# One large add with GELU: the arrays as three blocks in sequence, with an input parked in another's place

## The chip, the core and the metric

The kernel runs on one core of a Trainium2 chip. The inputs and the output lie in HBM; the core's compute engines read and write SBUF, an on-chip memory of 128 partitions, and 16 DMA engines move data between the two. Engines that matter here: DVE (VectorE) adds, ACT (ScalarE) computes the GELU, SP (SyncE) issues the transfers, POOL (GpSimd) takes part in the barriers and clears semaphores at the end.

The metric is the time of one execution on the device, in microseconds (us). The kernel before was run three times: 120.11 us median, 120.04 to 120.16.

## The reference

Two float32 arrays of 1024 x 4096 (16.78 MB each) are added, and the tanh form of the GELU is taken of each sum:

```python
def reference(x, y):
    z = x + y
    return (0.5 * z * (1 + np.tanh(np.sqrt(2 / np.pi) * (z + 0.044715 * z ** 3)))).astype(np.float32)
```

Every output element depends on the same element of x and of y alone. So any split of the elements into rows and blocks is allowed, if x, y and the output are split alike.

## The kernel before

**Tiling.** Each array is seen as 128 rows of TOT = 32,768 elements (8 rows of the array one after the other, 128 KB), one for each partition. The tile `zt` (128 x 32,768) holds x, then the sum, then the result, all in place. The tile `yt` (128 x 16,384) holds one half of y at a time; the second half of y goes where the first one was.

**Transfers.** All of them are issued by SP, in one queue, in the order of the list `sp`: the first half of y (64 KB a row), both halves of x (64 KB each), then the second half of y in two pieces (48 and 16 KB a row), then the two halves of the output (64 KB each). The functions are `load_x` (L123), `load_y` (L128) and `store` (L132). Seven transfers, each of 128 rows, eight rows for each of the 16 DMA engines.

**Compute.** The elements are cut into 17 chunks (`chunks`): fifteen of 2,048 and two of 1,024 elements a partition. `add` (L151) does x + y on DVE, `gelu` (L156) does the activation in place on ACT.

**Order.** The program is written out by hand inside `tc.manual_schedule()`: a loop takes from the lists `sp`, `acts` and `dve` whatever has its needs done already (`needs`), and so sets each engine's own order. Across engines only semaphores hold. The waits that matter on SP:

- the 48 KB piece of y waits for the first six adds, as it overwrites what they read; the 16 KB piece waits for the eighth;
- the first store waits for the eight gelus of the first half, and by the constant `GATE = 8` (L96) also for the ninth add, the first of the second half. That dependency is added by hand (L134) with the reason "the stores join the queue when the last load is nearly done";
- the second store waits for the last gelu.

Two edits of the finished instruction list frame this. `begin_early` moves the first two transfers on SP ahead of the barrier with which the program starts. `wait_late` takes the wait for the last transfer out of the closing barrier, so that the reset of the semaphores is done while the last store is still under way; ACT waits for that store alone, as the very last instruction.

A one-element GELU at the start (L183) loads ACT's table while the first loads run.

Of the kernel before, what the change touches and what calls it, by code (L numbers as in the profile page):

```python
# [8 lines left out]
def begin_early(nc, count):  # L9


    head, body = (b.instructions for b in nc.main_func.blocks[:2])
    SP = mybir.EngineType.SP
    moved = [i for i in body if i.engine == SP and isinstance(i, mybir.InstDMACopy)][:count]
    assert not any(i.sync_info and i.sync_info.on_wait for i in moved)
    assert all(i.regs_accessed() == ((), ()) for i in moved)
    at = next(k for k, i in enumerate(head) if i.engine == SP)
    for k, i in enumerate(moved):
        body.remove(i)
        head.insert(at + k, i)  # L20


def wait_late(nc):

    body, end = (b.instructions for b in nc.main_func.blocks[1:3])
    last = [i for i in body if isinstance(i, mybir.InstDMACopy)][-1]
    (sem,) = [u.id for u in last.sync_info.on_update]
    all_done = end[0]  # L30
    reset = next(i for i in end if isinstance(i, mybir.InstDrain) and i.is_reset_sema)
    at = end.index(reset)
    clear = end[at + 1]
    first, stop = reset.reset_range_start, reset.reset_range_stop
    assert all_done.engine == mybir.EngineType.SP and reset.engine == mybir.EngineType.Pool
    assert isinstance(clear, mybir.InstISA) and clear.engine == mybir.EngineType.Pool
    waits = all_done.sync_info.on_wait
    (its,) = [w for w in waits if w.id == sem]

    end[0] = mybir.InstDrain(  # L40
        name=all_done.name, engine=all_done.engine, debug=all_done.debug, is_reset_sema=False,
        sync_info=mybir.SyncInfo(on_wait=[w for w in waits if w.id != sem], on_update=[]),
    )
    parts = []
    for f, e in ((first, sem), (sem + 1, stop)):
        if f < e:
            nc.gpsimd.sem_clear(range(f, e))
            parts.append(nc.cur_bb.bb.instructions.pop())
    end[at + 1 : at + 2] = parts
    end.append(  # L50
        mybir.InstEventSemaphore(
            name=clear.name, engine=mybir.EngineType.Activation, debug=clear.debug,
            sync_info=mybir.SyncInfo(
                on_wait=[its],
                on_update=[
                    mybir.SyncUpdate(
                        sync_type="semaphore", id=sem, ant_name=its.ant_name,
                        update_mode="sem-sub-imm", update_value=its.wait_value,
                    )
                ],  # L60
            ),
        )
    )


@with_exitstack
def kernel(
    ctx: ExitStack,
    tc: tile.TileContext,
    x: bass.AP,  # L70
    y: bass.AP,
    out: bass.AP,
):

    nc = tc.nc
    P = nc.NUM_PARTITIONS  # L80
    fp32 = mybir.dt.float32
    act = mybir.ActivationFunctionType

    N, D = x.shape
    assert N % P == 0
    TOT = N // P * D
    xv, yv, ov = (a.rearrange("(p n) d -> p (n d)", p=P) for a in (x, y, out))

    HALF = TOT // 2
    xloads = [HALF, HALF]  # L90
    yloads = [16384, 12288, 4096]
    stores = [16384, 16384]
    chunks = [2048] * 15 + [1024, 1024]
    by_pool = []
    in_psum = []
    GATE = 8  # L96

    def ranges(sizes):
        ends = [sum(sizes[: i + 1]) for i in range(len(sizes))]
        assert ends[-1] == TOT  # L100
        return [(e - f, e) for e, f in zip(ends, sizes)]

    xr, yr, sr, cr = (ranges(r) for r in (xloads, yloads, stores, chunks))
    C = len(cr)
    second = next(c for c in range(C) if cr[c][0] == HALF)

    def over(rs, lo, hi):
        return [i for i, (a, b) in enumerate(rs) if a < hi and b > lo]

    pool_sb = ctx.enter_context(tc.tile_pool(name="xz", bufs=1))  # L110
    pool_y = ctx.enter_context(tc.tile_pool(name="y", bufs=1))
    pool_ps = ctx.enter_context(
        tc.tile_pool(name="ps", bufs=max(1, len(in_psum)), space=bass.MemoryType.PSUM)
    )

    one = pool_sb.tile([P, 992], fp32, tag="one", name="one")
    zt = pool_sb.tile([P, TOT], fp32, tag="z", name="z")
    yt = pool_y.tile([P, HALF], fp32, tag="y", name="y")
    xp, adds = {}, {}

    def load_x(i):
        a, b = xr[i]
        nc.sync.dma_start(out=zt[:, a:b], in_=xv[:, a:b])  # L123

    def load_y(i):
        a, b = yr[i]
        o = a % HALF
        nc.sync.dma_start(out=yt[:, o : o + b - a], in_=yv[:, a:b])  # L128

    def store(i):  # L130
        a, b = sr[i]
        ins = nc.sync.dma_start(out=ov[:, a:b], in_=zt[:, a:b])  # L132
        if i == 0 and GATE is not None:
            tc.add_manual_dep(  # L134
                ins.ins,
                adds[GATE].name,
                mybir.DependencyInfo(mybir.DependencyClass.Sync, mybir.DependencyReason.DATA),
                reason="the stores join the queue when the last load is nearly done",
            )

    def to_psum(c):
        a, b = cr[c]
        xp[c] = pool_ps.tile([P, 2048], fp32, tag="xp", name=f"xp{c}")
        nc.scalar.copy(out=xp[c][:, : b - a], in_=zt[:, a:b])

    def add(c):
        a, b = cr[c]
        o = a % HALF
        eng = nc.gpsimd if c in by_pool else nc.vector
        first = xp[c][:, : b - a] if c in in_psum else zt[:, a:b]  # L150
        ins = eng.tensor_add(out=zt[:, a:b], in0=first, in1=yt[:, o : o + b - a])  # L151
        adds[c] = ins.ins

    def gelu(c):
        a, b = cr[c]
        nc.scalar.activation(out=zt[:, a:b], in_=zt[:, a:b], func=act.Gelu_apprx_tanh)  # L156

    sp = [(load_y, i) for i in over(yr, 0, HALF)] + [(load_x, 0), (load_x, 1)]
    sp += [(load_y, i) for i in over(yr, HALF, TOT)]
    sp += [(store, i) for i in range(len(stores))]  # L160
    pool = [(add, c) for c in by_pool]
    dve = [(add, c) for c in range(C) if c not in by_pool]
    order = list(range(second, C))
    acts = [(gelu, c) for c in range(second)] + [(to_psum, c) for c in in_psum]
    acts += [(gelu, c) for c in order]
    assert sorted(order) == list(range(second, C))

    needs = {
        load_x: lambda i: [],
        load_y: lambda i: [(add, c) for c in over(cr, yr[i][0] - HALF, yr[i][1] - HALF)],  # L170
        to_psum: lambda c: [(load_x, i) for i in over(xr, *cr[c])],
        add: lambda c: [(load_x, i) for i in over(xr, *cr[c])]
        + [(load_y, i) for i in over(yr, *cr[c])]
        + [(to_psum, k) for k in in_psum if k == c],
        gelu: lambda c: [(add, c)],
        store: lambda i: [(gelu, c) for c in over(cr, *sr[i])]
        + ([(add, GATE)] if GATE is not None else []),
    }
    queues = [sp, pool, acts, dve]
    done = set()  # L180
    with tc.manual_schedule():
        nc.vector.memset(one[:, :1], 0.0)  # L182
        nc.scalar.activation(out=one[:, :1], in_=one[:, :1], func=act.Gelu_apprx_tanh)  # L183
        while any(queues):
            moved = False
            for q in queues:
                while q and all(n in done for n in needs[q[0][0]](q[0][1])):
                    fn, arg = q.pop(0)
                    fn(arg)
                    done.add((fn, arg))  # L190
                    moved = True
                    if q is not sp:
                        break
            assert moved, [q[:1] for q in queues]

    ctx.close()
    tc.close()
    tc.compile()  # L198
    begin_early(nc, 2)
    wait_late(nc)  # L200
# [30 lines left out]
```

## Time and profile before

One execution was profiled. Its own time and what else matters:

| | us |
|---|---|
| the profiled execution's own time | 120.19 |
| its span, from the first to the last of the program's instructions | 118.7 |
| DVE busy, 18 instructions | 35.5 |
| ACT busy, 19 instructions | 32.0 |
| idle time of DVE before its adds, ended by a landing of x | 40.0 |
| the same, ended by a landing of y | 16.2 |
| one add of 128 x 2,048, mean | 2.285 |
| one GELU of 128 x 2,048, mean | 1.910 |
| DMA engines' share of the span with packets | 98.5% |

How to read the profile: a line such as L151 is a line of the kernel's source. "SPq" is SP's sequencer, which waits and issues transfers. `z<-in_x_dram` is what an operation writes and reads, by the program's names. The row of digits for DMA has the span in 40 equal slices and gives the busy share of the 16 DMA engines in each, in tenths (9 is 90% or more). The trace also records every DMA packet with its start, duration and size; in this kernel one packet is one row of a transfer, and one more packet of 4 bytes for each DMA engine closes a transfer.

### The profile page before, as it was taken

The page shows a single profiled execution, that of the slowest core. Times are in us where ns is not written, and L with a number is a line of the kernel's source. Part 1 is how long each engine was busy: PE and PEld are TensorE (multiplying, and loading weights), DVE is VectorE, ACT ScalarE, POOL GpSimd, SP SyncE. Part 2 cuts the span into 40 slices and gives each one's busy share as a digit, 9 for nine tenths or more (in the row PEclk, how much of TensorE's full clock was granted, in tenths as well). Part 3 has the DMA queues.
Part 4 walks back from the last instruction along what each step waited for, and adds up shares of the span by engine and source line. Part 5 has one row for each costly group of instructions (what it writes and reads, how often), then busy time and mean ns, then how long its engine had stood idle before and what let it go on. Part 6 is the DMA issues. An engine that isn't in the chain of part 4 may idle for free.

```text
span 118.7 us, 96 instructions
## 1 busy us (share of the span) xinstructions
DVE 35.5 (30%) x18; ACT 32.0 (27%) x19; POOL 0.2 (0%) x4
## 2 busy tenths in 40 slices
DVE  0000000000000099999900000699999300000000
ACT  5000000000000029899850000079989800000000
POOL 0000000000000000000000000000000000000000
DMA  9889888998899888988898996998899889988890
GB/s 353 353 353 685 375 353 353 596 464 353 353 442 618 353 353 353 685 375 353 353 530 381 414 530 271 431 624 353 353 596 464 353 353 442 618 353 353 353 685 22
DMA packets 1008, 50.33 MB, mean 424 GB/s; under 512 B 112, under 2 KB 112, under 8 KB 112
## 3 DMA queue, kind: packets, MB, share of 16 engines
q1 hardware_dynamic: 1008, 50.33, 98.5%
HBM read 33.55 MB, written 16.78 MB: 424 GB/s over the span
## 4 chain that ended last, share of the span: by engine, by line
DMA 52%; DVE 22%; ACT 2%; DVEq 2%; ACTq 1%; SPq 0%; issue 0%
DMA z<-in_x_dram 34%; DVE z L151 22%; DMA y<-in_y_dram 17%; ACT z L156 2%; DVEq L198 2%; ACTq L198 1%; SPq L128 0%; DVEq L151 0%
## 5 line engine op out<-in xcount | busy, mean ns | idle before, releaser
L151 DVE TENSOR_TENSOR z<-z,y 128x2048 f32<-128x2048 f32 (+1 forms) x17 | 35.5, 2160 | 56.2 <-DMA z<-in_x_dram 40.0
L156 ACT ACTIVATE z<-z 128x2048 f32<-128x2048 f32 (+1 forms) x17 | 30.5, 1807 | 61.3 <-DVE z L151 61.3
L183 ACT ACT_TABLE_LOAD x1 | 1.3, 1283 | 1.3 <-PEq L215 1.3
L182 DVE MEMSET one<- 128x1 f32 x1 | 0.1, 59 | 1.3 <-PEq L215 1.3
L183 ACT ACTIVATE one<-one 128x1 f32<-128x1 f32 x1 | 0.2, 203 | 0.0
L215 POOL MEMSET const-bfloat16-1.0<- 128x1 bf16 x1 | 0.1, 101 | 0.0
L215 POOL MEMSET const-uint8-127<- 128x1 uint8 x1 | 0.1, 101 | 0.0
L215 POOL MEMSET const-float32-0.0<- 128x1 f32 x1 | 0.1, 98 | 0.2 <-issue 0.2
L215 POOL MEMSET const-float32-1.0<- 128x1 f32 x1 | 0.1, 98 | 0.0
## 6 DMA issues: line engine op xcount, KB each, us to landing
y<-in_y_dram SPq DMA_DIRECT2D x1, 6144.0 KB, 20.5
y<-in_y_dram SPq DMA_DIRECT2D x1, 2048.0 KB, 20.9
z<-in_x_dram SPq DMA_DIRECT2D x2, 50.1
out_dram<-z SPq DMA_DIRECT2D x2, 22.9
y<-in_y_dram SPq DMA_DIRECT2D x1, 22.0
```

Source lines behind the costliest of these rows:

```text
L151: ins = eng.tensor_add(out=zt[:, a:b], in0=first, in1=yt[:, o : o + b - a])
L156: nc.scalar.activation(out=zt[:, a:b], in_=zt[:, a:b], func=act.Gelu_apprx_tanh)
L182: nc.vector.memset(one[:, :1], 0.0)
L183: nc.scalar.activation(out=one[:, :1], in_=one[:, :1], func=act.Gelu_apprx_tanh)
L198: tc.compile()
L215: nc = _bacc.Bacc("TRN2", target_bir_lowering=False, num_devices=1)
```

## The change

The arrays are flattened, and cut into three blocks that follow each other in HBM. Block k is 128 rows of `LEN[k]` elements: 12,544, 7,680 and 12,544 (50,176, 30,720 and 50,176 bytes a row). A row goes to one partition. A transfer of a block thus covers one unbroken stretch of HBM, where before it took a piece out of each of 128 rows that lie 128 KB apart.

`yt` has room for y of blocks 1 and 2. y of block 0 is loaded into the place in `zt` that x of block 2 takes later (`y_at`). So y and x of block 0, x of block 1 and y of block 2 can be issued at once; x of block 2 waits until the seven adds of block 0 have read the parked y. Blocks are computed in the order 0, 2, 1, with seven, four (block 1) and seven pieces of 1,792, 1,920 and 1,792 elements. The stores are issued in the order 0, 2, 1; the first one also waits for the third add of block 2 (`GATE = (2, 2)`). Nine transfers replace seven.

In the instruction lists, SP's order becomes: y0, x0 (both ahead of the barrier), x1, y2, then x2 with a wait for DVE and for the landing of y0, y1, then the three stores with their waits. DVE has 18 adds where it had 17, ACT 18 gelus where it had 17. POOL clears its semaphores at the end with two instructions instead of one, since the semaphore of the last store no longer lies at the end of the range. `begin_early` and `wait_late` are unchanged.

```diff
-    xv, yv, ov = (a.rearrange("(p n) d -> p (n d)", p=P) for a in (x, y, out))
+    LEN = [12544, 7680, 12544]
+    PIECES = [7, 4, 7]
+    GATE = (2, 2)
+    AT = [sum(LEN[:k]) for k in range(3)]
-    xloads = [HALF, HALF]
-    yloads = [16384, 12288, 4096]
-    stores = [16384, 16384]
-    chunks = [2048] * 15 + [1024, 1024]
-    GATE = 8
+    def rows(a, k):
+        flat = a.rearrange("n d -> (n d)")
+        return flat[P * AT[k] : P * (AT[k] + LEN[k])].rearrange("(p c) -> p c", p=P)
...
     zt = pool_sb.tile([P, TOT], fp32, tag="z", name="z")
-    yt = pool_y.tile([P, HALF], fp32, tag="y", name="y")
+    yt = pool_sb.tile([P, LEN[1] + LEN[2]], fp32, tag="y", name="y")
+    def z(k, lo=0, hi=None):
+        return zt[:, AT[k] + lo : AT[k] + (LEN[k] if hi is None else hi)]
+    def y_at(k, lo=0, hi=None):
+        hi = LEN[k] if hi is None else hi
+        if k == 0:
+            return z(2, lo, hi)
+        o = 0 if k == 2 else LEN[2]
+        return yt[:, o + lo : o + hi]
+    def load_x(k):
+        nc.sync.dma_start(out=z(k), in_=rows(x, k))
+    def load_y(k):
+        nc.sync.dma_start(out=y_at(k), in_=rows(y, k))
+    def store(k, gate=None):
+        ins = nc.sync.dma_start(out=rows(out, k), in_=z(k))
+        if gate is not None:
+            tc.add_manual_dep(ins.ins, adds[gate].name, ...
+    def block(k):
+        for i in range(PIECES[k]):
+            lo, hi = i * step[k], (i + 1) * step[k]
+            v = z(k, lo, hi)
+            adds[k, i] = nc.vector.tensor_add(out=v, in0=v, in1=y_at(k, lo, hi)).ins
+            nc.scalar.activation(out=v, in_=v, func=act.Gelu_apprx_tanh)
...
+        load_y(0)
+        load_x(0)
+        load_x(1)
+        load_y(2)
+        block(0)
+        load_x(2)
+        load_y(1)
+        block(2)
+        store(0, GATE)
+        block(1)
+        store(2)
+        store(1)
```

## The prediction

> **What bounds the kernel now.** I read the page first, then the chain of waits, the SP queue in order of time, stretches of the span, and last the start and duration of every DMA packet in the trace.
>
> The page:
>
> ```profile
> span 118.7 us, 96 instructions
> ...
> DVE 35.5 (30%) x18; ACT 32.0 (27%) x19; POOL 0.2 (0%) x4
> ...
> DMA  9889888998899888988898996998899889988890
> ...
> q1 hardware_dynamic: 1008, 50.33, 98.5%
> HBM read 33.55 MB, written 16.78 MB: 424 GB/s over the span
> ```
>
> No compute engine is busy for a third of the span; the DMA engines are, for 98.5%. The digits hold 8 or 9 in nearly every slice: no stretch stands out in which the transfers ran dry.
>
> The chain that ended last, in order of time:
>
> ```profile
> 0.43 40.84 DMA z<-in_x_dram
> ...
> 41.37 13.31 DVE z L151 x6
> ...
> 54.70 20.47 DMA y<-in_y_dram
> ...
> 90.80 2.86 ACT z L156 x2
> 93.66 0.95 ACTq L198
> ```
>
> It follows computing instructions, so it stops at 94.6 us, 24 us before the end of the span. The rest is stores alone. Its DVE pieces look critical, yet a DVE piece costs time only if a DMA queue is empty meanwhile. So I look at when SP issues:
>
> ```profile
> 0.00 0.38 SPq L128 DMA_DIRECT2D y<-in_y_dram  x1
> 0.43 1.16 SPq L123 DMA_DIRECT2D z<-in_x_dram  x2
> 54.70 4.73 SPq L128 DMA_DIRECT2D y<-in_y_dram  x2
> 77.62 17.35 SPq L132 DMA_DIRECT2D out_dram<-z  x2
> ```
>
> and at the transfers in stretches (the last two columns are the DMA engines' share and GB/s; packets are booked where they start, so a share can pass 1):
>
> ```profile
> 5.00:41.00 36.00, 0.00 (x0) 0.00 (x0) 0.00 (x0) 1.00 1.01 437
> 41.00:79.00 38.00, 21.44 (x10) 16.69 (x9) 0.00 (x0) 1.00 0.96 413
> 79.00:116.00 37.00, 14.04 (x8) 13.85 (x9) 0.00 (x0) 1.00 1.05 454
> ```
>
> There is no slow stretch: loading alone, loading beside compute and storing differ by their edges only. The packet records settle it. Each of the 16 DMA engines moves 56 rows (of 64, 48 or 16 KB). A row of 65,536 B lasts 2,418 ns and the next begins 4 ns before its end, hence 2,414 ns a row; 49,152 B take 1,811.5 ns, 16,384 B 607 ns. The line through these is 4.7 ns + 0.036764 ns a byte. A transfer's closing 4-byte packet takes 5 ns, and the first row of the next transfer follows it without a gap, at every change of transfer, the change from loads to stores too. So the time before is, for the DMA engine that ends last: first packet at 1.79 us; its first row 0.52 us longer than the later ones (2,935 against 2,418 ns); then 40 x 2.414 + 8 x 1.8115 + 8 x 0.607 + 7 x 0.005 = 115.94 us. That makes 118.25; its recorded end is 118.31, and the wait on the last landing ends the span at 118.70. The profiled execution took 120.19 us, 1.49 of it outside the span; the median of the runs shown is 120.11, 0.08 lower.
>
> **The change part by part.**
>
> *Row sizes and number of transfers.* The 50.33 MB stay. Nine transfers replace seven, with 72 rows per DMA engine in place of 56. By the line, a row of 50,176 B takes 1,849.4 ns and one of 30,720 B 1,134.1 ns. Eight rows of each transfer: 8 x (6 x 1.8494 + 3 x 1.1341) + 9 x 0.005 = 116.03 us, against 115.94: +0.09 us. It is 16 more rows at 4.7 ns and two more closing packets at 5 ns. All of this is on the path.
>
> The Trainium skill, "DMA: Bandwidth & Descriptors", section "Anatomy of one DMA", gives (for transfers from GpSimd's path) a fit of about 2.0 us fixed and bytes / 436e3 us for each DMA, which speaks against two more transfers: charged in full, an estimate of +4.0 us. The joints recorded here show 5 ns where transfers queue behind each other, so the measurement decides.
>
> *Addresses.* Before, neighbouring rows lie 131,072 B apart in HBM; after, a transfer reads or writes one unbroken region with rows 50,176 or 30,720 B apart. The trace has no row at such a pitch. Bound above: a group of rows that start near 55 and 57 us lasted up to 2,434 ns; the usual one of the slowest dozen, 2,432, is 14 over 2,418, and as a steady price that is 48 rows' worth of 64 KB x 0.014 = +0.67 us. Bound below: 0, since loads and stores alike run at 2,418 ns and nothing in the records shows a row under 2,415. I take 0, by the nearest rows: the 48 and 16 KB rows lie on the same line, so the rate follows bytes.
>
> [...]
>
> *The start.* Both kernels put two loads ahead of the barrier, 128 rows each, so I leave the first packets where they are (1.01 to 1.79 us over the 16 DMA engines, 1.79 the one that ends last). First rows lasted 2,822 to 3,362 ns, 404 to 944 over a later row. Start plus excess is when a DMA engine is up to speed: 1.66 for the quickest, 1.92 in the mean, 2.31 for the last. Bounds: all as early as the quickest, -0.65 us; the last one with the largest excess, +0.43. I take 0, as the two are nearly balanced and the row nearest is the kernel's own.
>
> *The waits of SP.* First, the loads. y0, x0, x1 and y2 are issued without a wait (before: y0, x0, x1). x of block 2 now waits for all seven adds of block 0, since y0 lies in its place; y of block 1 and the stores are behind it. With 2.31 us for the start, y0 ends at 17.1, x0 at 31.9, x1 at 41.0, y2 at 55.8 on the last DMA engine, 0.66 earlier on the first. A landing is seen 0.36 after the last packet (21.62 against 21.98 for the first transfer), so adds start near 32.4. An add of 2,048 starts every 2.20 us, and 1,024 took 1.14 to 1.15: 1.94 for 1,792. The seventh ends near 46.0. x2 is issued there, and the queue holds work until 55.1. An issue reaches an idle queue after 1.01 to 1.79 us (the first load), so 7 us of cover are left. If it went, every us late is a us.
>
> Second, the gate. x2 ends at 70.6, is seen at 70.95; the third add of block 2 ends near 77.0, and store 0 is issued. The last load, y1, ends at 79.0 on the first DMA engine and 79.7 on the last: 2.0 us of cover against 1.01 needed. Before: issue at 77.62, cover until 79.02, 1.4 us, and no gap. Store 0's gelus are over near 48.
>
> Third, the other stores. Adds of block 2 end near 84.6, its last gelu near 86.4 (1.91 us for 2,048); store 2 has until 93.8. Block 1's four adds (2.07 each) end near 92.9, its gelus near 95; store 1 has until 108.6. Cost 0.
>
> *DVE and ACT.* 18 adds replace 17, over the same elements; all of it lies under transfers, as shown. Cost 0; its cover is gone only if the margins above are.
>
> *The end.* Before, the reset of the semaphores waited for the first store and was over at 100.1 us. After, it waits for store 2 (landed near 109.6) and POOL clears two ranges instead of one, a 77 ns instruction; over near 110.4, 8 us before the last store lands. Cost 0.
>
> Sum: +0.09 us. On the profiled execution's 120.19 that is 120.28; on the median of 120.11 it is 120.20, which I predict. About 0.2%, 0.24 us, is what a measurement of this kernel can tell from no change; the sum is below it.
>
> **The rivals.**
>
> *A quicker start.* For it: first rows were 404 to 944 ns too long while later ones vary by some ns, and the DMA engines that started first were held up most, as if 16 equal pitches got in each other's way. Against: the last DMA engine has only 517 of excess, and its late first packet need not move. If all are up to speed at the mean, 1.92: -0.39 + 0.09 = -0.30, so 119.81.
>
> *Slower: the new pitch costs in every row.* For it: no row of before lies at this pitch. Against: three row sizes on one line. At the slowest later row, +0.67 + 0.09: 120.87. It decides from 3.2 ns per 64 KB (0.15 / 48), since 0.09 + 0.15 is the 0.24.
>
> *Slower: a bubble at the gate or at x2.* Every us that store 0 comes over 1.04 late is a us; with one add more in front of it (1.94), +0.9 + 0.09: 121.1. Against: more cover than before's 1.4.
>
> *The change does nothing measurable:* the forecast itself.
>
> **How the numbers follow.** Forecast (within 0.24 us of before): 0.47. Quicker start: 0.28, all faster. New pitch: 0.17; bubble or another cost of the additional transfers: 0.08; both slower. So faster 0.28, same 0.47, slower 0.25. The range, 119.75 to 120.75, takes in the quicker start and most of the pitch's price; left out are the start's extreme, the pitch in full and the bubble. The likeliest case alone reaches from 119.9 to 120.35.
>
> **What would show it.** Right: DMA shares of 8 and 9 throughout and 98% on the queue; x2 issued near 46, store 0 near 77, store 2 near 86, store 1 near 95; rows of 1,853 and 1,138 ns (4 more than the step); a span near 118.8. A quicker start shows in the first rows' excess and in the last DMA engine's first packet; the pitch in the later rows; a bubble as a slice under 8 near 55 or 79. The prediction is wrong if rows aren't on the line, if a joint costs more than 5 ns, or if the 1.49 us outside the span move.

## The result, and the profile after

The changed kernel takes 121.06 us (median of 6, 120.95 to 121.18) where the kernel before took 120.10 (median of 6). The ratio is 1.008, 95% interval 1.0067 to 1.0093: slower by 0.8%, some 0.96 us. The forecast was 120.2 with a range of 119.75 to 120.75, so the time lies 0.3 us outside it. The profiled execution took 121.02 us, 1.49 of it outside the span, exactly as before.

The page of the changed kernel:

```profile
span 119.5 us, 105 instructions
...
DVE 35.6 (30%) x19; ACT 32.5 (27%) x20; POOL 0.2 (0%) x4
...
DMA  8989989899899998998999989999999899898994
...
q1 hardware_dynamic: 1296, 50.33, 98.0%
HBM read 33.55 MB, written 16.78 MB: 421 GB/s over the span
```

Nothing here points at a stage. The digits (busy share of the DMA engines in each fortieth of the span, in tenths) are 8 and 9 up to the last one, which is 4: in the last 3 us some DMA engines have stopped already. The queue of SP, and the transfers in stretches (last two columns: the DMA engines' share, GB/s):

```profile
0.00 0.38 SPq L120 DMA_DIRECT2D z<-in_y_dram  x1
0.43 1.16 SPq L117 DMA_DIRECT2D z<-in_x_dram  x2
1.64 0.66 SPq L120 DMA_DIRECT2D y<-in_y_dram  x1
46.74 0.33 SPq L117 DMA_DIRECT2D z<-in_x_dram  x1
47.12 0.43 SPq L120 DMA_DIRECT2D y<-in_y_dram  x1
77.83 18.15 SPq L123 DMA_DIRECT2D out_dram<-z  x3
```

```profile
5.00:41.00 36.00, 7.92 (x5) 5.15 (x4) 0.00 (x0) 1.00 1.01 435
41.00:79.00 38.00, 12.85 (x7) 11.32 (x7) 0.00 (x0) 1.00 0.99 428
79.00:116.00 37.00, 14.78 (x8) 14.49 (x9) 0.00 (x0) 1.00 1.01 435
116.00:119.50 3.50, 0.00 (x0) 0.00 (x0) 0.00 (x0) 1.00 0.45 193
```

The waits of SP end 0.6 to 1.3 us behind the forecast (x2 at 46.7 against 46, store 0 at 77.8 against 77, store 2 at 87.3 against 86, store 1 at 95.6 against 95), and the long stretches run at 428 to 435 GB/s. The time was lost before 5 us. The issues of the first transfer, with the time from issue to landing, show it first (kernel before, rows of 64 KB; then the changed kernel, rows of 49 KB):

```profile
y<-in_y_dram SPq DMA_DIRECT2D x1, 22.0
```

```profile
z<-in_y_dram SPq DMA_DIRECT2D x1, 6272.0 KB, 18.1
```

The first transfer was to be complete at 17.1 + 0.36 = 17.5 us. It took 18.1. A landing is made of one report from each of the 16 DMA engines, and the trace keeps all of them. This table, which is no view of the profile, is worked out from those reports (us from the start of the span):

```
                          first transfer            last transfer
                    earliest  latest  spread   earliest  latest  spread
before (64 KB rows)   21.30    21.98   0.69     117.98   118.66   0.68
after  (49 KB rows)   16.78    18.14   1.36     118.11   119.49   1.38
```

The DMA engines start apart and stay apart: the spread of 1.36 us is still 1.38 some 101 us later, so nothing evens it out, and the one that comes up last ends last. From the packet records, where a row's excess is what it lasts longer than later rows of its size: in the changed kernel the first rows began at 1.01 to 2.73 us (before: 1.01 to 1.79) and had an excess of 19 to 1,789 ns (before: 404 to 944). Start plus excess, the moment when a DMA engine is up to speed, is 2.99 us for the last one, against 2.31 before; its last packet ends 116.08 us later, at 119.07, against 116.00 before. Averaged over the 16 the excess is the same, 704 against 695 ns, and the first rows begin 0.17 us later (1.39 against 1.22 us). So the mean DMA engine is up to speed 0.18 us later (2.10 against 1.92) and the last one 0.68: most of it is waiting that falls on few. The last one began early, at 1.20 us; it has the longest first row.

So the 0.83 us by which the span grew are 0.68 at the start, 0.08 for the additional rows, and 0.08 by which the end of the span came later behind the last packet (0.46, before 0.38); each of the three is rounded.

### The profile page after: what moved, and what is told of

It is laid out like the page before. It is cut to its first block, busy times and chain, and to the rows that moved or that the text cites. A ratio compares the mean times of both kernels' runs of the same rounds, so it can differ in the third digit from the quotient of the medians.

```text
span 119.5 us, 105 instructions
## 1 busy us (share of the span) xinstructions
DVE 35.6 (30%) x19; ACT 32.5 (27%) x20; POOL 0.2 (0%) x4
## 4 chain that ended last, share of the span: by engine, by line
DMA 48%; DVE 28%; DVEq 2%; ACT 2%; issue 0%; SPq 0%
DMA z<-in_x_dram 48%; DVE z L136 28%; DVEq L157 2%; ACT z L137 2%; SPq L120 0%; DVEq L136 0%
## 5 line engine op out<-in xcount | busy, mean ns | idle before, releaser
L137 ACT ACTIVATE z<-z 128x1792 f32<-128x1792 f32 (+1 forms) x18 | 31.0, 1720 | 61.9 <-DVE z L136 61.9
L136 DVE TENSOR_TENSOR z<-z,y 128x1792 f32<-128x1792 f32 (+1 forms) x11 | 21.9, 2066 | 25.2 <-DMA z<-in_x_dram 25.2
L136 DVE TENSOR_TENSOR z<-z 128x1792 f32<-128x1792 f32 x7 | 13.6, 2019 | 31.7 <-DMA z<-in_x_dram 31.7
## 6 DMA issues: line engine op xcount, KB each, us to landing
z<-in_y_dram SPq DMA_DIRECT2D x1, 6272.0 KB, 18.1
```

What stands on the lines that cost most here:

```text
L136: adds[k, i] = nc.vector.tensor_add(out=v, in0=v, in1=y_at(k, lo, hi)).ins
L137: nc.scalar.activation(out=v, in_=v, func=act.Gelu_apprx_tanh)
```

## The experiments

What could have spoiled the start? The changed kernel differs there in three things: a fourth transfer is issued in the first 2.3 us (theory Issue); rows lie 50,176 B apart in HBM instead of 131,072 (theory Pitch); rows are 49 KB long instead of 64 (theory Row size). Each of the first four kernels changes one of them. "Up to speed" is again start plus excess, and each ratio is against the kernel before, timed again beside the run (medians of 120.02 to 120.04 us).

The first four runs are from one chip, the next four from a second, the other seven from a third. On each of the three, a first transfer at a pitch of 128 KB started evenly (spreads of 0.43 to 0.58 us), and one at 49 or 52 KB with rows of that length unevenly (1.19 to 1.39).

**Three loads first.** In the changed kernel, y of block 2 waits for the first add (`load_y` is given a second argument for this dependency).

```diff
...
-        load_y(2)
         block(0)
+        load_y(2, (0, 0))
```

> The changed kernel, except that the fourth load (y of block 2) waits for the first add and is issued near 33 us instead of 1.64; the queue holds work until 41. Theory Issue (the fourth transfer, issued while the first rows are still on their way, is what slowed the start): the DMA engine that is last is up to speed near 2.3 us again instead of 2.99, and the time falls by 0.6 to 0.7 us from 121.06, to about 120.4. Theory Pitch (rows 50,176 B apart in one stretch of HBM start slower) and theory Row size (a first row of 49 KB starts slower than one of 64): no change, 121.0 to 121.1, last one up to speed near 3.0.

Measured: 121.09 us, ratio 1.0083 (1.0067 to 1.0099). The transfer was issued where it was meant to be,

```profile
0.00 0.37 SPq L120 DMA_DIRECT2D z<-in_y_dram  x1
0.42 1.16 SPq L117 DMA_DIRECT2D z<-in_x_dram  x2
35.10 0.33 SPq L120 DMA_DIRECT2D y<-in_y_dram  x1
...
z<-in_y_dram SPq DMA_DIRECT2D x1, 6272.0 KB, 18.1
```

and the last DMA engine was up to speed at 2.96, the spread of the first landing 1.39 us: no better than in the changed kernel. Theory Issue falls.

**Same rows, old pitch.**

```diff
-        flat = a.rearrange("n d -> (n d)")
-        return flat[P * AT[k] : P * (AT[k] + LEN[k])].rearrange("(p c) -> p c", p=P)
+        return a.rearrange("(p n) d -> p (n d)", p=P)[:, AT[k] : AT[k] + LEN[k]]
```

> The changed kernel with rows of the same lengths, but taken out of 128 rows that lie 131,072 B apart, as before. Theory Pitch: the start is as before, about 120.2 to 120.4. Theory Issue and theory Row size: no change, 121.0 to 121.1.

Measured: 120.26 us, ratio 1.0015 (1.0002 to 1.0029). With nothing but addresses in HBM changed, the loss shrinks from 0.96 to some 0.2 us, of which 0.09 are the additional rows. The first transfer is complete 0.7 us earlier than in the changed kernel:

```profile
z<-in_y_dram SPq DMA_DIRECT2D x1, 6272.0 KB, 17.4
```

Row size falls as the cause by itself, as do the parked y, the new pieces and the order of the blocks: this kernel has them all. Theory Pitch stands. The spread of the first landing is 0.57 us here.

**Unbroken stretches with 64 KB rows.** The kernel before, with each array as two blocks in sequence.

```diff
-    xv, yv, ov = (a.rearrange("(p n) d -> p (n d)", p=P) for a in (x, y, out))
...
+    def rows(v, a, b):
+        h = a // HALF
+        half = v.rearrange("n d -> (n d)")[P * HALF * h : P * HALF * (h + 1)]
+        return half.rearrange("(p c) -> p c", p=P)[:, a - h * HALF : b - h * HALF]
...
```

> The kernel before with each array as two blocks in sequence in HBM: rows of 64 KB that lie 65,536 B apart, everything else as it was, three loads issued at the start. Theory Pitch: slower, by up to 0.7 us, if it is the unbroken stretch that costs; no change if only a pitch off the power of two does. Theory Issue and theory Row size: 120.1, no change.

Measured: 120.13 us, ratio 1.0005 (0.9994 to 1.0016). An unbroken stretch as such costs nothing that this can tell; a pitch of 65,536 B starts like one of 131,072 (up to speed at 2.35 us, before 2.31).

**Four transfers first, in the kernel before.**

```diff
-    xloads = [HALF, HALF]
+    xloads = [HALF, HALF // 2, HALF // 2]
...
```

> The kernel before with the second load of x cut in two transfers of 32 KB a row, so that four are issued in the first 2.3 us. Eight more rows and one more closing packet a DMA engine: +0.04 us. Theory Issue: +0.5 to +0.7 us on top, about 120.7 to 120.8, the last DMA engine up to speed near 2.9. Theory Pitch and theory Row size: 120.15.

Measured: 120.11 us, ratio 1.0006 (0.9997 to 1.0015). Theory Issue a second time: no.

**Which pitches?** The next four ask what about 50,176 B is bad: that it isn't a power of two (Spacing), or that rows start on a multiple of 1 KB only (Alignment), and whether it matters after the first transfer.

Rows of 52 KB, then of 56 KB, in unbroken stretches:

```diff
-    LEN = [12544, 7680, 12544]
-    PIECES = [7, 4, 7]
-    GATE = (2, 2)
+    LEN = [13312, 6144, 13312]
+    PIECES = [8, 3, 8]
+    GATE = (2, 1)
```

> The changed kernel with blocks of 13,312, 6,144 and 13,312 elements a row: rows of 53,248 B (13 x 4 KB) in one unbroken stretch, 72 rows a DMA engine as in the changed kernel; the pieces and the gate are moved to fit. Theory Spacing (any pitch that is not a power of two lets some DMA engines wait at the start while others run): about 121.0, the last DMA engine up to speed near 3. Theory Alignment (rows that start on a multiple of 1 KB only): about 120.2, since all rows start on 4 KB; the last one up to speed near 2.2.

```diff
-    LEN = [12544, 7680, 12544]
-    PIECES = [7, 4, 7]
-    GATE = (2, 2)
+    LEN = [14336, 4096, 14336]
+    PIECES = [7, 2, 7]
+    GATE = (2, 0)
```

> As the run with 52 KB rows, with 14,336, 4,096 and 14,336 elements: rows of 57,344 B (7 x 8 KB). Theory Spacing: about 121.0. Theory Alignment: about 120.2. Time in between the two would say that it is a matter of degree, by the power of two in the pitch.

Measured: 121.00 us (ratio 1.008, 1.0065 to 1.0094) and 120.35 (1.0018, 1.0006 to 1.003). Starting on 4 KB does not help at 52 KB, so Alignment falls; 56 KB is no power of two and is good, so Spacing in its plain form falls too.

Rows at the old pitch, with block 0 shifted to start on a multiple of 1 KB:

```diff
-        flat = a.rearrange("n d -> (n d)")
-        return flat[P * AT[k] : P * (AT[k] + LEN[k])].rearrange("(p c) -> p c", p=P)
+        at = [LEN[2], LEN[2] + LEN[0], 0][k]
+        return a.rearrange("(p n) d -> p (n d)", p=P)[:, at : at + LEN[k]]
```

> Rows of the changed kernel's lengths at a pitch of 131,072 B, with the block that is loaded first shifted by 50,176 B within its row: it starts on a multiple of 1 KB only. Theory Spacing: 120.26 as without the shift. Theory Alignment: about 121.0.

Measured: 120.24 us, ratio 1.0016 (1.0001 to 1.0031), spread of the first landing 0.45. Alignment falls a second time.

Block 0, and one half of the middle block beside it, at a pitch of 64 KB; block 2 (number 3 in this kernel) left at 50,176 B:

```diff
-    LEN = [12544, 7680, 12544]
-    PIECES = [7, 4, 7]
...
+    LEN = [12544, 3840, 3840, 12544]
+    PIECES = [7, 2, 2, 7]
...
+    HALF = TOT // 2
...
+        if k < 2:
+            return flat[: P * HALF].rearrange("(p c) -> p c", p=P)[:, AT[k] : AT[k] + LEN[k]]
         return flat[P * AT[k] : P * (AT[k] + LEN[k])].rearrange("(p c) -> p c", p=P)
...
```

> Block 0, whose y and x are the first two transfers, is taken from rows 65,536 B apart; block 2 keeps rows 50,176 B apart in one stretch; the middle block is two of 3,840 elements a row, one in what block 0 leaves of its rows, one unbroken. Twelve transfers and 96 rows a DMA engine: 24 rows x 4.7 ns + 3 x 5 = +0.13 us over the changed kernel's nine and 72. If only the pitch of the first transfer counts: 120.26 + 0.13 = 120.4. If the pitch of 50,176 B costs in the later transfers too: between that and 121.06 + 0.13 = 121.2.

Measured: 120.45 us, ratio 1.0033 (1.002 to 1.0046): the sum of 120.26 and 0.13 for three more transfers and 24 more rows, to 0.06. The first transfer was complete at

```profile
z<-in_y_dram SPq DMA_DIRECT2D x1, 6272.0 KB, 17.2
```

with a spread of 0.37 us, and the last with 0.35. Block 2, loaded and stored at 50,176 B later on, adds no more than those 0.06. It is the pitch of the transfers at the start that costs. The first two and a half of the middle block changed together here; that the loss is in the very first one is read from its landing, not from a run that changes it alone.

**A rule for the pitch?** After eight runs the power of two that divides the pitch fitted (8 KB for 56, more for 64 and 128; 4 and 1 KB for 52 and 49). The mixed kernel lets the pitch of block 0 be set apart from the length of its rows, here and in the next runs by one number (and the lengths and pieces of the middle block to fit). The next three forms are shown against the mixed kernel:

```diff
-    LEN = [12544, 3840, 3840, 12544]
-    PIECES = [7, 2, 2, 7]
-    HALF = TOT // 2
...
+    LEN = [12544, 2816, 4864, 12544]
+    PIECES = [7, 2, 4, 7]
...
+    HALF = 15360
```

> The mixed kernel (120.45 with block 0 taken from rows 65,536 B apart) with block 0 and the part beside it taken from rows 61,440 B apart (15 x 4 KB); the lengths of block 0's rows stay 50,176 B, transfers and rows stay 12 and 96. Theory Divisor (a pitch that a larger power of two divides starts evenly: 8 KB in 56 KB, and 64 and 128 KB are even; 4 KB in 52 KB and 1 KB in 49 KB uneven): 121.2. Theory Small pitch (pitches under some 54 KB start unevenly, whatever divides them): 120.45.

Measured: 121.00 us, ratio 1.0073 (1.005 to 1.0095). Same lengths of block 0's rows, same number of transfers and rows as with a pitch of 64 KB, and 0.55 us slower. (The mixed kernel itself was not timed again on this run's chip.) The first transfer again:

```profile
z<-in_y_dram SPq DMA_DIRECT2D x1, 6272.0 KB, 18.0
```

The spread of its landing, 1.20 us, is there at the end (1.20).

With `LEN = [12544, 768, 6912, 12544]`, `PIECES = [7, 1, 4, 7]` and `HALF = 13312`:

> The same with rows 53,248 B apart (13 x 4 KB); rows themselves stay 50,176 B long, so pitch and length are apart. Both theories: 121.2. Were it the length of the rows or the unbroken stretch that counts: 120.45.

Measured: 120.79 us, ratio 1.0061 (1.0039 to 1.0082). It is 0.34 us slower than at the 64 KB pitch, but less than the 0.75 or so that rows of 52 KB cost at the same pitch (121.00 against 120.26). So one pitch does not give one loss: what the rows' length or the rest of the layout adds is not told apart here.

For a pitch of 100 KB blocks 0 and 2 lie beside each other:

```diff
-    LEN = [12544, 3840, 3840, 12544]
-    PIECES = [7, 2, 2, 7]
-    HALF = TOT // 2
...
+    LEN = [12544, 512, 7168, 12544]
+    PIECES = [7, 1, 4, 7]
...
+    HALF = 25600
...
-        if k < 2:
-            return flat[: P * HALF].rearrange("(p c) -> p c", p=P)[:, AT[k] : AT[k] + LEN[k]]
-        return flat[P * AT[k] : P * (AT[k] + LEN[k])].rearrange("(p c) -> p c", p=P)
+        if k != 2:
+            at = {0: 0, 3: LEN[0], 1: LEN[0] + LEN[3]}[k]
+            return flat[: P * HALF].rearrange("(p c) -> p c", p=P)[:, at : at + LEN[k]]
+        return flat[P * HALF :].rearrange("(p c) -> p c", p=P)
```

> The same with blocks 0 and 2 and a part of the middle one taken from rows 102,400 B apart (25 x 4 KB). Theory Divisor: 121.2. Theory Small pitch: 120.45.

Measured: 120.69 us, ratio 1.0054 (1.0033 to 1.0076), 0.24 over the 64 KB pitch. Not small pitches alone, then; but a third of the 0.75 that the Divisor theory named.

**Second load held back, in the kernel before.** Only the first load is issued ahead of the barrier; the second waits for the warming activation.

```diff
...
+        if i == 0:
+            tc.add_manual_dep(ins.ins, warm.name, ...
...
-    begin_early(nc, 2)
+    begin_early(nc, 1)
```

> The kernel before with only the first load ahead of the barrier; the second waits for the warming activation and is issued near 2.8 us, the queue has work until 21. If the issue of the next transfers holds up the first rows (first rows are 0.4 to 0.9 us longer than later ones in the kernel before): up to 0.4 us faster than 120.04. If the first rows are slow by themselves: no change.

Measured: 120.04 us, ratio 1.0003 (0.9986 to 1.002), the second load issued at 2.31 us. The first rows' excess is 138 to 1,113 ns, so they are slow with no other transfer issued before 2.31 us.

**Nine times 8 KB, and seventeen times 4.** `LEN = [12544, 5888, 1792, 12544]`, `PIECES = [7, 4, 1, 7]`, `HALF = 18432`:

> The mixed kernel with block 0 and the part beside it taken from rows 73,728 B apart (9 x 8 KB), 12 transfers and 96 rows as in its other forms. Theory Divisor, with 8 KB already enough: as with 65,536 B, 120.45. If 56 KB was even for another reason than the 8 KB that divides it: 120.7 to 121.0.

and `LEN = [12544, 4864, 2816, 12544]`, `PIECES = [7, 4, 2, 7]`, `HALF = 17408`:

> The same with rows 69,632 B apart (17 x 4 KB). Theory Divisor: uneven, 120.7 to 121.0. Theory that pitches of 56 KB up to some 90 KB are even, apart from 60: 120.45.

Measured: 120.64 us (ratio 1.0049, 1.0036 to 1.0062) and 120.78 (1.0058, 1.0044 to 1.0071). Rows 72 KB apart lose 0.19 us against 64 KB, rows 68 KB apart 0.33. The 72 KB lie between the two numbers that were told apart, so the Divisor theory with a threshold at 8 KB isn't confirmed.

**A short transfer ahead of all.**

```diff
...
+        nc.sync.dma_start(
+            out=first[:16, :], in_=x.rearrange("(p n) d -> p (n d)", p=16)[:, :128]
+        )
         load_y(0)
...
-    begin_early(nc, 2)
+    begin_early(nc, 3)
```

> The changed kernel with one transfer more ahead of all others: one row of 512 B for each DMA engine, into a tile that nothing reads. The loads are issued some 0.43 us later for it. Theory Cold start (the first packets of a DMA engine are uneven at this pitch, whatever they carry): the first large rows then are even, and the time is 120.25 + 0.43 = 120.7. Theory Meeting (the 16 long rows that begin together at this pitch hold each other up): the unevenness stays, 121.06 + 0.43 = 121.5, or 121.1 where the row of 512 B hides the delay.

Measured: 121.38 us, ratio 1.0114 (1.01 to 1.0128). The short transfer and the first long one:

```profile
first<-in_x_dram SPq DMA_DIRECT2D x1, 8.0 KB, 1.8
...
z<-in_y_dram SPq DMA_DIRECT2D x1, 6272.0 KB, 18.2
```

The 512 B rows took 25 ns each. The long rows behind them lost 19 to 1,515 ns, and their landing is spread over 1.34 us. So it isn't a DMA engine's first packet, whatever it carries, that is uneven. What is left is the first long rows at this pitch; that they hold each other up, as theory Meeting has it, fits but was not tested by itself.

All runs but the one with the short transfer, by their groups. "Up" is when the last DMA engine was up to speed, "spread" that of the first long transfer's landing, both from the one profiled execution, whose own time is up to 0.2 us off the median; "less rows" is the median of the runs less 4.7 ns for each row of a DMA engine and 5 ns for each transfer that the kernel has over the 56 and 7 of before:

```
kernel             pitch of the      up    spread   time    less rows
                   first transfer    us      us      us        us
before_four_first  128 KB           2.06    0.43   120.11    120.07
before_one_first   128 KB           2.14    0.58   120.04    120.04
before             128 KB           2.31    0.69   120.10    120.10
before_contig       64 KB           2.35    0.77   120.13    120.13
strided_shift      128 KB           2.01    0.45   120.24    120.15
after_strided      128 KB           2.22    0.57   120.26    120.17
mixed               64 KB           2.04    0.37   120.45    120.24
after_56k           56 KB           2.37    0.71   120.35    120.26
mixed_72k           72 KB           2.49    0.91   120.64    120.43
mixed_100k         100 KB           2.45    0.92   120.69    120.48
mixed_68k           68 KB           2.71    0.99   120.78    120.57
mixed_52k           52 KB           2.44    0.79   120.79    120.58
mixed_60k           60 KB           2.90    1.20   121.00    120.79
after_52k           52 KB           2.74    1.19   121.00    120.91
after               49 KB           2.99    1.36   121.06    120.97
after_three_first   49 KB           2.96    1.39   121.09    121.00
```

Powers of two and 56 KB stand together, 120.04 to 120.26; all others are above, from 120.43 to 121.00. No kernel was faster than the one before, by the ratios: the lowest is 1.0003.

The first rows are not all of it. In the runs with pitches of 68 and 52 KB (mixed_68k, after_52k) second rows of the first transfer had an excess of up to 431 and 379 ns too, and in after_strided single rows half-way had up to 172; there the spread is 0.57 us at the first landing and 0.81 at the last.

## Why the prediction was wrong

- **The start** is the step that failed: "Both kernels put two loads ahead of the barrier, 128 rows each, so I leave the first packets where they are", and "I take 0". The term was +0.68 us, beyond its upper bound of +0.43. Number of transfers and rows were taken as what sets the first packets; the same-rows kernel at the old pitch shows that the addresses do, since giving the old addresses back returns 0.80 of the 0.96 us. The bound was built from first rows of the kernel before, and all of those lay at one pitch: it let the last DMA engine have the largest excess there, 944 ns, where the changed kernel's largest is 1,789.
- **Addresses.** The steady price of 0 was right: rows last 1,853 ns, as forecast, and the mixed kernel pays at most 0.06 us for block 2 at 50,176 B. (Two readings of the bound were off without effect: the slowest later row of the kernel before lasted 2,461 ns, not 2,434, and 0.15 / 48 is 3.1 ns, not 3.2.) The price was asked for in the wrong place, spread over all rows instead of at the first.
- **A quicker start**, the rival held likelier than any slower one, had the sign reversed. It read the long excess of the first rows as 16 equal pitches that get in each other's way. At the new pitch the mean excess stays at 0.70 us and falls on a few. The Trainium skill, "DMA: Bandwidth & Descriptors", section "Latency and other measured facts", advises padding the pitch off large powers of two by a few KiB, from copies at 512 KiB and more. No run here has such pitches; 4 KB more than 64 KB, the nearest to that advice, took 0.33 us longer (120.78 against 120.45).
- **Row sizes and number of transfers** held: +0.08 us measured from up to speed to the last packet, +0.09 forecast; 1,853 and 1,138 ns a row; and +0.13 forecast for the mixed kernel came out at +0.19. The same page's section "Anatomy of one DMA" gives a fixed 2.0 us for each transfer, on GpSimd's path. Behind SP's full queue they do not show: two more transfers and 16 more rows for each DMA engine cost the 0.08 us above.
- **The waits of SP** held but for 0.6 to 1.3 us, most of it the later start. The packets of the changed kernel follow each other without a gap, at the gate and at x2 too, so the rival of a bubble falls; that its 121.1 lies near the measured time is luck. **DVE, ACT and the time outside** the span cost nothing, as said. **The end** cost 0.08 us that were not forecast: the span ends 0.46 us after the last packet instead of 0.38. Why was not tried; over all runs it is 0.36 to 0.51, and 0.38 in the changed kernel with three loads first, so it need not belong to the change.

What stays open is the cause behind the pitch. It is shown that the first long rows at some pitches come up unevenly, that a short transfer ahead of them does not help, and that neither the issue of other transfers nor alignment makes it. The rows' length does not make it at 128 KB, where rows of 49 and of 64 KB start alike; at 52 KB two lengths came out 0.33 us apart (120.58 and 120.91, additional rows taken off). Why some pitches do it is not shown: no view here sees HBM from within, and the order 56, 72, 100, 68, 52, 60, 49 KB gives no rule clean enough to name a threshold.

## What to carry to other kernels

In a kernel like this one, bound by its transfers from end to end, what a DMA engine loses at the start it does not win back: the spread of the first transfer's landing was still there at the end, to 0.03 us in the two kernels compared and to 0.25 us in every run. Look at that spread before looking at any mean. Where the layout of the first transfer is free, take a pitch that has been measured (here 64 or 128 KB), and treat the start as a term with bounds of its own when addresses change, even where steady rows show no price.

## What the runs showed of the hardware that was not expected

The earliest of the 16 DMA engines was not late in any run: with rows of 49 KB and nothing ahead of them its share of the first transfer landed at 16.7 to 16.9 us at every pitch, while the latest came between 17.18 and 18.14. How close behind the first load the next ones are issued makes no difference that shows, in either kernel (120.11 and 120.04 against 120.02, 121.09 against 121.06). And a transfer of one 512 B row for each DMA engine, put ahead of the rest, cost 0.32 us (121.38 against 121.06), though its rows last 25 ns; it puts off the issue of the first load from 0.00 to 0.44 us.
